# Where tiles start in SBUF: moving operands of the dense products at 0 modulo 256 bytes, small rings shortened

## The chip, the cores and the metric

The kernel runs on one NeuronCore of a Trainium2 chip. The metric is the device time of one execution in microseconds; of several executions the median counts. TensorE is called PE below, its weight loads PEld, VectorE DVE, ScalarE ACT, GpSimd POOL and SyncE SP.

## The reference

Two transformer-like blocks follow each other on 256 tokens of width 1024, batch 1, all in float32. The first block has two layers. Layer 0 joins a differential attention and a gated convolution of width 31; layer 1 joins a state-space model and a latent attention. Each layer then has a gated feed-forward part of width 2816. The second block has two layers with two streams (`x`, and a context `ctx` of 256 tokens): modulation by a conditioning vector, a windowed attention beside a grouped-query attention, a gated merge and again a gated feed-forward part.

```
def sandwich(x, g_pre, g_post, fn):
    return x + rmsnorm(fn(rmsnorm(x, g_pre)), g_post)

def swiglu(h, w_gate, w_up, w_down):
    return (jax.nn.silu(h @ w_gate) * (h @ w_up)) @ w_down

def branch_merge(ya, yb, ga, gb, w_pa, w_pb, w_o):
    merged = jax.nn.sigmoid(ga) * (ya @ w_pa) + jax.nn.sigmoid(gb) * (yb @ w_pb)
    return merged @ w_o
```

What matters here are the dense products with the weight matrices. Nearly all of PE's work is such a product of 256 tokens with a 128 x 128 piece of a weight matrix.

## The kernel before

**One dense product.** Activations lie with their features on the 128 partitions and the 256 tokens along the free axis. Weights arrive in 1 MB pieces as float32 in a ring of three `raw` tiles. `need` (line 333) cuts a piece into units of up to 128 x 1024 and splits each: ACT writes the rounded high half `uh` (line 349), DVE the rest `ul` (line 350), each in a ring of three. The activations are split likewise into a high and a low tile. `mm3` (line 363) makes one 128 x 256 output out of three matmuls of one k-tile, which the text calls a triple:

```
mm(ps, lhsT=wh, rhs=ah, start=start, stop=False)
mm(ps, lhsT=wh, rhs=al, start=False, stop=False)
mm(ps, lhsT=wl, rhs=ah, start=False, stop=stop)
```

`rhs` is the moving operand, which streams through the array; `lhsT` is the stationary operand, which a weight load brings in ahead of it. They are lines 369, 370 and 371. There are 4130 triples, and the order of the work around them is set by a table of step counts (`ORDER`) that interleaves queues of steps.

**The moving operands.** By the names in the trace: `xacth`/`xactl` (the split activations of stream x, 2192 triples), `slot` (the same for the context stream in the arena `ar`, 896), `hh`/`hl` (the hidden values of a feed-forward part, 704), `xmh`/`xml` and `xyg`/`xyn` (attention results, 256 together), `cacth` (context activations late in the second block, 48) and `nqh`, `nkvh` (34). In `token_steps` (lines 827 to 829) the roles are turned: the weights move (512 columns) and the activations are stationary.

**The rest of PE's work** is plain float32: attention scores (line 1861), transposes of probabilities (line 893), products with values (lines 901, 1891), modulation (line 1657) and statistics (lines 417, 423).

**Where a tile lies.** Tiles come from pools (`main`, `work`, `ar`, `ph`, `s5`, `ck`) that are stacked in SBUF; a tag's ring takes its place when its first tile is asked for, in steps of 32 bytes. So the start of every tile follows from the sizes and the order of all tiles asked for before it. No line of the kernel names an address.

Of the kernel before, what the change touches and what calls it, by code (L numbers as in the profile page):

```python
# [17 lines left out]
P = 128  # L18
# [134 lines left out]
class Kern:  # L153
# [20 lines left out]
    def __init__(self, ctx, tc, ins, out):  # L174
        self.ctx, self.tc, self.nc, self.ins, self.out = ctx, tc, tc.nc, ins, out
        self.cnt = 0
        self.pools = {}
        self.later, self.held, self.key = [], [], None


# [37 lines left out]
    def setup(self):  # L218
        nc, tc, ctx = self.nc, self.tc, self.ctx
        self.psum = ctx.enter_context(tc.tile_pool(name="psum", bufs=1, space=PSUM))  # L220
        ctx.callback(lambda: [self.close(k) for k in list(self.pools)[::-1]])
        self.open("main")
        self.consts = self.sb("main", "consts", [P, CBASE])
        self.vecs = self.sb("main", "vecs", [P, VSPLIT])
        self.ones = self.sb("main", "ones", [P, P])
        nc.gpsimd.memset(self.ones, 1.0)
        nc.sync.dma_start(self.consts[:, 0:P], self.ins["consts"][:, 0:P])
        nc.sync.dma_start(self.vecs[:, 0:KD], self.ins["vectors"][:, 0:KD])
        c = lambda k: self.consts[:, COFF[k][0]:COFF[k][0] + COFF[k][1]]
        self.ident, self.hsel, self.nmask = c("ident"), c("hsel"), c("nmask")  # L230
# [104 lines left out]
    def need(self, u, ahead=None):  # L335
        while self.uptr < len(self.units) and self.uptr <= u.idx + (self.UNIT_AHEAD if ahead is None else ahead):
            q = self.units[self.uptr]
            if not self.load_to(q.raw.idx):
                assert self.uptr > u.idx
                break  # L340
            self.load_to(q.raw.idx + self.RAW_AHEAD)
            self.uptr += 1
            src = q.raw.t[:, q.k0:q.k1, q.c0:q.c1]
            nk, ncol = q.k1 - q.k0, q.c1 - q.c0
            h = self.sb("main", "uh", [P, 1024], F32R, bufs=self.UNIT_BUFS)
            l = self.sb("main", "ul", [P, 1024], F32R, bufs=self.UNIT_BUFS)
            q.h = h[:, :nk * ncol].rearrange("p (k c) -> p k c", c=ncol)
            q.l = l[:, :nk * ncol].rearrange("p (k c) -> p k c", c=ncol)
            self.nc.scalar.activation(q.h, src, AF.Copy)  # L349
            self.nc.vector.tensor_tensor(q.l, src, q.h.bitcast(F32), ALU.subtract)  # L350
            self.used(q.raw)
        return u
# [48 lines left out]
    def rsqrt_small(self, ssum, n, dim, epsj=0):  # L401

        nc = self.nc
        e = lambda t: self.sb("work", "rs_" + t, [P, 16], bufs=4)[:, :n]
        v, y = e("v"), e("y0")
# [338 lines left out]
    def swiglu(self, st, wg, wu, cg, cu, wd, evacs, R=True):  # L744
# [14 lines left out]
        def rstd_a():  # L759
            st["rs"] = self.stats_a(st.pop("acc"), D)  # L760
            st["late"] = self.sb("ph", "late", [P, 2])
            self.nc.vector.tensor_copy(st["late"], st["rs"])
# [89 lines left out]
    def softmax(self, ps, groups, scale, keys, d, it, pre=None, tile=None):  # L852


        nc = self.nc
        mx = self.sb("work", "mx", [P, 2], bufs=4)[:, :groups]
        nm = self.sb("work", "nm", [P, 2], bufs=4)[:, :groups]
        sm = self.sb("work", "sm", [P, 2], bufs=8)[:, :groups]
        pt = (tile or self.w2)("prob", [P, 512])[:, :groups * keys].rearrange("p (g k) -> p g k", g=groups)
# [68 lines left out]
    def even_mixer(self, st):  # L928
# [6 lines left out]
        def begin():  # L935
            self.open("ph")
            s["C"], s["S"] = self.table("ph", "dc"), self.table("ph", "ds")
            s["u"] = self.sb("ph", "u", [P, 4, 30 + T])
            nc.gpsimd.memset(s["u"][:, :, 0:30], 0.0)
            s["cy"] = self.sb("ph", "cy", [P, 4, T])  # L940
            s["q"] = self.sb("ph", "q", [P, 4, T])
            s["k"] = self.sb("ph", "k", [P, 4, T])
            s["v"] = self.sb("ph", "v", [P, 2, 512])

        def lam():
# [3 lines left out]
            n = self.ps("n")  # L949
            nc.tensor.matmul(n[:, 0:2], lhsT=self.ones, rhs=pr, start=True, stop=True)  # L950
            e = self.sb("ph", "le", [P, 2])
# [103 lines left out]
        def weights(it):  # L1055
            K = P if it[0] == 0 else T
            self.undefer((id(d), it))
            pt, sm = d[it]
            ri = self.recip(sm)
            r1 = self.sb("work", "r1", [P, 1], bufs=2)  # L1060
            nc.vector.tensor_tensor(r1, ri[:, 1:2], s["nlam"], ALU.mult)
            wt = self.sb("work", "wt", [P, T], bufs=2)[:, :K]
            nc.vector.tensor_scalar(wt, pt[:, 1, :], r1, None, ALU.mult)
            nc.vector.scalar_tensor_tensor(wt, pt[:, 0, :], ri[:, 0:1], wt, ALU.mult, ALU.add)
            d[it] = wt
# [5 lines left out]
        def out(it):  # L1071
# [4 lines left out]
            if h == 0:  # L1076
                s["ss", qt] = self.sb("work", "ssq", [P, 4], bufs=2)
                s["ot", qt] = two("ot", [P, 512])
# [109 lines left out]
    def s5_setup(self, s):  # L1188
# [7 lines left out]
        def disc():  # L1196
# [9 lines left out]
            mag = yield from self.pexp("s5t", v, 8, "pm")  # L1206
            s["mag"] = self.sb("s5", "mag", [P, 8])
            nc.vector.tensor_copy(s["mag"], mag)
# [137 lines left out]
    def odd_mixer(self, st, s):  # L1346
# [124 lines left out]
        def glu():  # L1471
            ps = self.ps("d").rearrange("p (a t) -> p a t", a=2)
            za = [(s["zh"][:, k, :], s["zl"][:, k, :]) for k in range(2)]
            for a in range(2):
                self.dense(ps[:, a, :], [ug], za, c0=P * a)
            hb = self.sb("ph", "hb", [P, 2])
            nc.vector.tensor_scalar(hb, self.vec("l1_b_glu", 0, 2), 0.5, None, ALU.mult)
# [149 lines left out]
    def mod_setup(self):  # L1627
# [3 lines left out]
        def fn():  # L1631
            self.cs = self.sb("main", "cs", [P, KD, 32])
            nc.gpsimd.memset(self.cs, 0.0)
            t = self.sb("work", "ct", [P, 2 * KD])
            for i, n in enumerate(("c_2", "c_ctx_2")):
# [3 lines left out]
                nc.vector.tensor_tensor(self.cs[:, :, i], g, v, ALU.mult)  # L1639
            self.mods = {}  # L1640

        return [Step(fn)]

    def mod_steps(self, l):
# [4 lines left out]
        def big(c, r):  # L1649
            if c == 0:  # L1650
                m["t"] = self.mods[l] = self.sb("main", f"mod{l}", [P, 48, 2])
                m["g"] = self.mods[l, "g"] = self.sb("main", f"modg{l}", [P, 2, KD, 2])
            ps = self.ps("d")[:, :256]
# [102 lines left out]
    def proj_steps(self, st, l, rope, queries=True):  # L1756
# [22 lines left out]
        def nk(i, ps):  # L1779
            if i == 0:  # L1780
                self.new_kv(st, ("nk", "nv"))
            nc.scalar.activation(st["nk"][:, 2 * i:2 * i + 2, :], ps[0], AF.Copy)

# [274 lines left out]
    def second_block(self, X, C):  # L2058
# [6 lines left out]
        def tables(l):  # L2065
            if l == 0:
                self.open("ck", "right")
                self.new_kv(keys[0], ("gk", "gv", "nk", "nv"))
                for k in ("gk", "gv", "nk", "nv"):
                    self.unspill(keys[0], k, keys[0][k])  # L2070
# [75 lines left out]
    def prep_ctx(self, C):  # L2146
# [33 lines left out]
        def end():  # L2180
            self.spill(C, "x1", C["x"])
            C["rs1"] = self.sb("main", "crs", [P, 2])
            nc.vector.tensor_copy(C["rs1"], self.stats_a(C.pop("acc"), D))
# [46 lines left out]
    def chains(self):  # L2230
# [6 lines left out]
        self.prep_ctx(C)  # L2237
        main = [Step(lambda: self.open("work")), Step(lambda: self.open("ar"))] + self.first_block(X)
        for k in "dc":
# [32 lines left out]
```

## Time and profile before

| | us |
|---|---|
| median of 3 runs | 2039.46 (2037.99 to 2041.78) |
| the profiled execution | 2035.8 |
| its span, first to last instruction | 2034.0 |
| PE busy, share of the span | 95% |
| DVE busy | 67% |
| ACT busy | 49% |
| mean granted TensorE clock | 0.978 |

The span leaves 1.8 us of the profiled execution's own time outside. Matmuls overlap in the pipe, so a busy PE does not say at which pace they come; the distance between the starts of two matmuls does. Views that name a tile give the first and last start of a group and how many there were.

### The profile page before, as it was taken

To read this page: it belongs to the slowest core of one execution; us is meant where nothing else is said; L and a number is where in the kernel's file an instruction comes from. 1 tells how busy PE (TensorE), PEld (TensorE's weight loads), DVE (VectorE), ACT (ScalarE), POOL (GpSimd) and SP (SyncE) were. 2 spreads that over 40 slices of the span, in tenths; PEclk is the share of its full clock that TensorE was granted. 3 is DMA by queue.
4 is the path that set the end of the run, shared out by engine and by line. 5 is a ranking of instruction groups with operands and counts; after the bars stand their busy time and mean duration, and the time that the engine had idled before them with its cause. 6 is when DMAs were issued, how large, how long until landed. Compare 5 with 4: busy or idle time off the path is not lost.

```text
span 2034.0 us, 38003 instructions
## 1 busy us (share of the span) xinstructions
PE 1927.8 (95%) x15646; PEld 1785.2 (88%) x15646; DVE 1361.2 (67%) x2655; ACT 988.7 (49%) x1680; POOL 71.9 (4%) x112
## 2 busy tenths in 40 slices
PE   8889999999989999989996999989999899979998
PEld 7678889999878999789996888889999888879998
DVE  6997668777778678666655745676655755566554
ACT  5355665444445453554443455445444455535443
POOL 0212000000000000000001100000000100000000
PEclk9999999999989999999998999999999999999999
DMA  7756636666748665766556633345555643244553
GB/s 255 247 193 207 195 110 201 202 218 220 230 133 241 205 187 141 236 200 217 194 174 188 156 101 86 122 145 173 182 175 199 159 120 89 81 149 158 179 177 109
DMA packets 383775, 353.51 MB, mean 174 GB/s; under 512 B 14705, under 2 KB 370545, under 8 KB 383089
## 3 DMA queue, kind: packets, MB, share of 16 engines
q1 hardware_dynamic: 378336, 333.77, 51.9%
q0 software_dynamic: 4688, 15.73, 3.3%
q8 instruction: 123, 2.02, 0.4%
q10 hardware_dynamic: 576, 1.57, 0.2%
q14 instruction: 52, 0.42, 0.1%
HBM read 344.36 MB, written 6.68 MB: 173 GB/s over the span
## 4 chain that ended last, share of the span: by engine, by line
PE 76%; DVE 14%; ACT 4%; DMA 4%; issue 2%; SPq 0%; ACTq 0%; DVEq 0%
PE psd L369 21%; PE psd L371 20%; PE psd L370 20%; DVE ul L350 4%; PE pss L1861 4%; ACT uh L349 3%; PE pss L893 2%; PE psn L1891 2%; DMA raw<-in_w_in 2%; DVE cy L999 1%; PE psd L1657 1%; DMA raw<-in_l_w_in 1%; DMA raw<-in_w_mod 1%; PE psd L827 1%; DVE xres L592 1%
## 5 line engine op out<-in xcount | busy, mean ns | idle before, releaser
L350 DVE TENSOR_TENSOR ul<-raw,uh 128x1024 fp32r<-128x1024 f32 (+3 forms) x556 | 657.5, 1190 | 365.3 <-ACT uh L349 363.3
L349 ACT ACTIVATE uh<-raw 128x1024 fp32r<-128x1024 f32 (+3 forms) x556 | 566.0, 1025 | 337.1 <-PE psd L370 272.3
L369 PE MATMUL psd<-xacth,uh 128*128 128x256 f32 x2192 | 633.9, 289 | 9.9 <-ACT grp L703 3.1
L371 PE MATMUL psd<-xacth,ul 128*128 128x256 f32 x2192 | 626.2, 286 | 5.1 <-DVE ul L350 5.1
L370 PE MATMUL psd<-xactl,uh 128*128 128x256 f32 x2192 | 626.2, 286 | 0.6 <-DVE xactl L599 0.5
L369 PEld LDWEIGHTS psd<-xacth,uh 128*128 128x128 f32 x2192 | 425.8, 194 | 28.2 <-issue 13.4
L371 PEld LDWEIGHTS psd<-xacth,ul 128*128 128x128 f32 x2192 | 425.9, 194 | 6.6 <-DVE ul L350 6.5
L370 PEld LDWEIGHTS psd<-xactl,uh 128*128 128x128 f32 x2192 | 426.0, 194 | 1.9 <-DVE xactl L599 1.0
L369 PE MATMUL psd<-slot,uh 128*128 128x256 f32 x896 | 256.0, 286 | 0.5 <-ACT uh L349 0.5
L371 PE MATMUL psd<-slot,ul 128*128 128x256 f32 x896 | 251.4, 281 | 2.6 <-DVE ul L350 2.6
L370 PE MATMUL psd<-slot,uh 128*128 128x256 f32 x896 | 251.0, 280 | 0.0
L371 PE MATMUL psd<-hh,ul 128*128 128x256 f32 x704 | 198.1, 281 | 0.6 <-DVE ul L350 0.3
L369 PE MATMUL psd<-hh,uh 128*128 128x256 f32 x704 | 198.0, 281 | 0.0
L370 PE MATMUL psd<-hl,uh 128*128 128x256 f32 x704 | 197.5, 280 | 0.0
L369 PEld LDWEIGHTS psd<-slot,uh 128*128 128x128 f32 x896 | 169.6, 189 | 7.4 <-issue 5.2
L371 PEld LDWEIGHTS psd<-slot,ul 128*128 128x128 f32 x896 | 169.3, 189 | 3.3 <-DVE ul L350 3.3
L370 PEld LDWEIGHTS psd<-slot,uh 128*128 128x128 f32 x896 | 169.4, 189 | 0.0
L371 PEld LDWEIGHTS psd<-hh,ul 128*128 128x128 f32 x704 | 132.0, 188 | 1.6 <-DVE ul L350 1.6
L369 PEld LDWEIGHTS psd<-hh,uh 128*128 128x128 f32 x704 | 132.5, 188 | 0.4 <-issue 0.4
L370 PEld LDWEIGHTS psd<-hl,uh 128*128 128x128 f32 x704 | 132.5, 188 | 0.0
L869 ACT ACTIVATE prob<-pss,nm 128x512 f32<-128x512 f32 (+2 forms) x124 | 70.2, 568 | 22.3 <-DVE nm L879 18.9
L875 DVE TENSOR_REDUCE mx<-pss 128x1 f32<-128x512 f32 (+1 forms) x80 | 55.2, 689 | 34.4 <-PE pss L1861 33.2
(480 smaller groups left out, 2528.4 us busy)
## 6 DMA issues: line engine op xcount, KB each, us to landing
raw<-in_w_mod SPq DMA_DIRECT2D x48, 1024.0 KB, 5.5
raw<-in_w_ffn_in SPq DMA_DIRECT2D x40, 1024.0 KB, 5.1
raw<-in_w_in SPq DMA_DIRECT2D x32, 1024.0 KB, 5.7
raw<-in_w_ffn_in SPq DMA_DIRECT2D x52, 512.0 KB, 5.2
raw<-in_w_in SPq DMA_DIRECT2D x48, 512.0 KB, 5.2
raw<-in_w_ffn_out SPq DMA_DIRECT2D x24, 1024.0 KB, 4.9
raw<-in_l_w_gate SPq DMA_DIRECT2D x20, 1024.0 KB, 5.3
raw<-in_l_w_up SPq DMA_DIRECT2D x20, 1024.0 KB, 5.3
```

What stands on the lines that cost most here:

```text
L349: self.nc.scalar.activation(q.h, src, AF.Copy)
L350: self.nc.vector.tensor_tensor(q.l, src, q.h.bitcast(F32), ALU.subtract)
L369: mm(ps, lhsT=wh, rhs=ah, start=start, stop=False)
L370: mm(ps, lhsT=wh, rhs=al, start=False, stop=False)
L371: mm(ps, lhsT=wl, rhs=ah, start=False, stop=stop)
L592: nc.vector.tensor_tensor(x(m), x(m), d.pop(m), ALU.add)
L827: mm(d[i][j], lhsT=ah[:, s], rhs=u.h[:, k, :], start=kk == 0, stop=False)
L869: nc.scalar.activation(pt[:, g, :], ps[:, g, :] if one else ps[g], AF.Exp, bias=nm[:, g:g + 1], scale=scale, accum_out=sm[:, g:g + 1])
L875: nc.vector.tensor_reduce(mx, ps, AX.X, ALU.max)
L893: self.nc.tensor.transpose(t[:, k * P:(k + 1) * P], w[:, k * P:(k + 1) * P], self.ident)
L1861: nc.tensor.matmul(ps[:, a, T * i:T * i + T], lhsT=q, rhs=k, start=True, stop=True)
L1891: nc.tensor.matmul(o[64 * a:64 * a + 64, 0, g, :], lhsT=kv[kind + "v"][:, k, c:c + 64], rhs=two[a][0][:, P * i:P * i + P], start=i == 0, s ...
```

## The change

It asks for small tiles in another place and order, shortens some rings, and adds padding, so that the big tiles start elsewhere. Five small tiles move from other pools to the head of `main` (`cs`, `mag`, `crs`, the modulation tables, the rings `sm`, `mx`, `ssq`); the tile of ones shrinks from 128 columns to one, which a matmul now reads with a broadcast; `rs_a`, `rs_b`, `rs_y1`, `rs_y2` have three buffers instead of four; `r1`, `ct`, `hb` and `late` use rings of the same size that exist already; padding stands before `uh`, in `work` and in `ck`.

On all five engines the instructions stand in the same order as before, and each waits for the same counts of the same semaphores. What differs is where operands lie (and the width of one memset). From the two built programs, start address modulo 256 bytes (the moving slices are 1024 bytes apart, the stationary ones 512):

| tile | before | now |
|---|---|---|
| `uh`, `ul` (split weights) | 192 | 192 |
| `xacth`, `xactl` | 192 | 0 |
| `slot` (all), `xmh`, `xml`, `xyg`, `xyn` | 0 | 0 |
| `hh`, `hl` in layer 0 of the first block (176 triples) | 64 | 0 |
| `hh`, `hl` in layer 1 of the first block (176 triples) | 32 | 0 |
| `hh`, `hl` in the second block (352 triples) | 0 | 0 |
| `cacth`, `cactl` | 224 | 0 |
| `nqh`, `nql`, `nkvh`, `nkvl` | 32 | 0 |
| `raw` | 192 | 0 |
| rings of `work` (`w1`, `w2`, `acc`) | 224 | 0 |

Modulo 512 the split weights go from 448 to 192, `xacth` from 448 to 0, and `slot` and the second block's `hh` stay at 256.

```diff
@@ -176,6 +176,7 @@
+        self.cut = False
@@ -222,7 +223,18 @@
-        self.ones = self.sb("main", "ones", [P, P])
+        self.ones = self.sb("main", "ones", [P, 1])
+        self.cs = self.sb("main", "cs", [P, KD, 32])
+        self.mag = self.sb("main", "mag", [P, 8])
+        self.crs = self.sb("main", "crs", [P, 2])
+        self.mods = {}
+        for l in range(2):
+            self.mods[l] = self.sb("main", f"mod{l}", [P, 48, 2])
+            self.mods[l, "g"] = self.sb("main", f"modg{l}", [P, 2, KD, 2])
+        for tag, n, bufs in (("sm", 2, 8), ("mx", 2, 4), ("ssq", 4, 2)):
+            self.sb("main", tag, [P, n], bufs=bufs)
+        self.sb("main", "pad", [P, 8])
@@ -342,6 +354,10 @@
+            if self.uptr == 1 and not self.cut:
+                self.cut = True
+                self.sb("main", "upad", [P, 48])
@@ -401,7 +417,7 @@
-        e = lambda t: self.sb("work", "rs_" + t, [P, 16], bufs=4)[:, :n]
+        e = lambda t: self.sb("work", "rs_" + t, [P, 16], bufs=4 if t in ("v", "y0", "y3") else 3)[:, :n]
@@ -758,7 +774,7 @@
-            st["late"] = self.sb("ph", "late", [P, 2])
+            st["late"] = self.sb("work", "keep", [P, 2])
@@ -853,9 +869,9 @@
-        mx = self.sb("work", "mx", [P, 2], bufs=4)[:, :groups]
+        mx = self.sb("main", "mx", [P, 2], bufs=4)[:, :groups]
-        sm = self.sb("work", "sm", [P, 2], bufs=8)[:, :groups]
+        sm = self.sb("main", "sm", [P, 2], bufs=8)[:, :groups]
@@ -935,19 +951,19 @@
-            s["u"] = self.sb("ph", "u", [P, 4, 30 + T])
-            nc.gpsimd.memset(s["u"][:, :, 0:30], 0.0)
+            s["u"] = self.sb("ph", "u", [P, 4, 30 + T])
+            nc.gpsimd.memset(s["u"][:, :, 0:30], 0.0)
-            nc.tensor.matmul(n[:, 0:2], lhsT=self.ones, rhs=pr, start=True, stop=True)
+            nc.tensor.matmul(n[:, 0:2], lhsT=self.ones.to_broadcast([P, P]), rhs=pr, start=True, stop=True)
@@ -1057,7 +1073,7 @@
-            r1 = self.sb("work", "r1", [P, 1], bufs=2)
+            r1 = self.sb("main", "mx", [P, 2], bufs=4)[:, :1]
@@ -1074,7 +1090,7 @@
-                s["ss", qt] = self.sb("work", "ssq", [P, 4], bufs=2)
+                s["ss", qt] = self.sb("main", "ssq", [P, 4], bufs=2)
@@ -1204,7 +1220,7 @@
-            s["mag"] = self.sb("s5", "mag", [P, 8])
+            s["mag"] = self.mag
@@ -1473,7 +1489,7 @@
-            hb = self.sb("ph", "hb", [P, 2])
+            hb = self.sb("work", "mu", [P, 2])
@@ -1629,15 +1645,13 @@
-            self.cs = self.sb("main", "cs", [P, KD, 32])
-            t = self.sb("work", "ct", [P, 2 * KD])
+            t = self.sb("work", "rs_v", [P, 16], bufs=4)
-            self.mods = {}
@@ -1648,8 +1662,7 @@
-                m["t"] = self.mods[l] = self.sb("main", f"mod{l}", [P, 48, 2])
-                m["g"] = self.mods[l, "g"] = self.sb("main", f"modg{l}", [P, 2, KD, 2])
+                m["t"], m["g"] = self.mods[l], self.mods[l, "g"]
@@ -1779,6 +1792,8 @@
+                if st.get("pn") == "ck":
+                    self.sb("ck", "pad", [P, 248])
@@ -2066,6 +2081,7 @@
+                self.sb("ck", "pad", [P, 248])
@@ -2179,7 +2195,7 @@
-            C["rs1"] = self.sb("main", "crs", [P, 2])
+            C["rs1"] = self.crs
@@ -2235,7 +2251,7 @@
-        main = [Step(lambda: self.open("work")), Step(lambda: self.open("ar"))] + self.first_block(X)
+        main = [Step(lambda: (self.open("work"), self.sb("work", "pad", [P, 16]))), Step(lambda: self.open("ar"))] + self.first_block(X)
```

## Rows read from the trace of the kernel before

**Rows 1.** The page: span, then busy us, share, instructions of the engines.
```profile
span 2034.0 us, 38003 instructions
...
PE 1927.8 (95%) x15646; PEld 1785.2 (88%) x15646; DVE 1361.2 (67%) x2655; ACT 988.7 (49%) x1680; POOL 71.9 (4%) x112
```

**Rows 2.** The page, chain that ended last: shares by engine, then by line.
```profile
PE 76%; DVE 14%; ACT 4%; DMA 4%; issue 2%; SPq 0%; ACTq 0%; DVEq 0%
PE psd L369 21%; PE psd L371 20%; PE psd L370 20%; DVE ul L350 4%; PE pss L1861 4%; ACT uh L349 3%; PE pss L893 2%; PE psn L1891 2%; DMA raw<-in_w_in 2%; DVE cy L999 1%; PE psd L1657 1%; DMA raw<-in_l_w_in 1%; DMA raw<-in_w_mod 1%; PE psd L827 1%; DVE xres L592 1%
```

**Rows 3.** The page, costliest groups: count, busy us, mean ns, idle before.
```profile
L369 PE MATMUL psd<-xacth,uh 128*128 128x256 f32 x2192 | 633.9, 289 | 9.9 <-ACT grp L703 3.1
...
L369 PE MATMUL psd<-slot,uh 128*128 128x256 f32 x896 | 256.0, 286 | 0.5 <-ACT uh L349 0.5
...
L369 PE MATMUL psd<-hh,uh 128*128 128x256 f32 x704 | 198.0, 281 | 0.0
```

**Rows 4.** View of tile xacth, 1880:1940 (192 modulo 256): ns min/median/max, first and last start.
```profile
L371 PE MATMUL psd<-xacth,ul x168: 283/283/283, 1879.7 to 1939.8; 128*128 128x256 f32 x168
```

**Rows 5.** View of tile hh, 1982:2012, second block (0 modulo 256).
```profile
L369 PE MATMUL psd<-hh,uh x86: 279/279/279, 1981.8 to 2011.8; 128*128 128x256 f32 x86
```

**Rows 6.** View of tile slot, 639:651 (0 modulo 256).
```profile
L370 PE MATMUL psd<-slot,uh x35: 279/279/279, 638.8 to 650.8; 128*128 128x256 f32 x35
```

**Rows 7.** View of tile hh, 1064:1084, layer 1 (32 modulo 256).
```profile
L369 PE MATMUL psd<-hh,uh x56: 279/282/286, 1063.9 to 1083.7; 128*128 128x256 f32 x56
```

**Rows 8.** View of tile hh, 368:386, layer 0 (64 modulo 256).
```profile
L369 PE MATMUL psd<-hh,uh x31: 279/281/285, 367.7 to 378.4; 128*128 128x256 f32 x31
```

**Rows 9.** View of tile slot, three windows with shorter matmuls (0 modulo 256).
```profile
L370 PE MATMUL psd<-slot,uh x22: 276/276/276, 128.9 to 138.7; 128*128 128x256 f32 x22
L370 PE MATMUL psd<-slot,uh x40: 276/276/283, 534.2 to 550.8; 128*128 128x256 f32 x40
L370 PE MATMUL psd<-slot,uh x14: 276/276/276, 692.4 to 696.9; 128*128 128x256 f32 x14
```

**Rows 10.** Windows: engines busy us (count), granted clock, DMA share, GB/s.
```profile
core 0: us, PE busy (x) PEld busy (x) DVE busy (x) ACT busy (x) POOL busy (x), PEclk, DMA share, GB/s
639.00:651.00 12.00, 12.00 (x104) 12.00 (x104) 7.65 (x11) 5.75 (x9) 0.00 (x0) 1.00 0.84 229
692.60:697.00 4.40, 4.40 (x41) 4.40 (x41) 2.85 (x6) 1.98 (x2) 0.00 (x0) 1.00 0.88 247
1064.00:1084.00 20.00, 20.00 (x169) 20.00 (x168) 10.33 (x11) 9.55 (x14) 0.00 (x0) 1.00 0.52 171
1880.00:1940.00 60.00, 60.00 (x503) 60.00 (x502) 35.11 (x36) 27.26 (x32) 0.00 (x0) 1.00 0.58 190
1982.00:2012.00 30.00, 30.00 (x257) 30.00 (x256) 16.75 (x20) 12.15 (x15) 0.00 (x0) 1.00 0.50 164
```

**Rows 11.** View of line L1703 on DVE: operands at 192 (xact) and 0 (slot).
```profile
L1703 DVE SCALAR_TENSOR_TENSOR xactl<-nt,mod,xacth x32: 475/477/486, 1116.8 to 1834.3; 128x256 fp32r<-128x256 f32 x32
L1703 DVE SCALAR_TENSOR_TENSOR slot<-nt,mod,slot x16: 476/477/482, 104.8 to 631.1; 128x256 fp32r<-128x256 f32 x16
```

**Rows 12.** View of line L1861, 1200:1300 (xnk at 224).
```profile
L1861 PE MATMUL pss<-xnk,xnq x32: 376/428/480, 1234.4 to 1291.8; 64*128 64x256 f32 x32
```

**Rows 13.** View of line L1861, 1640:1780 (xnk at 0).
```profile
L1861 PE MATMUL pss<-xnk,xnq x32: 376/428/481, 1703.1 to 1758.2; 64*128 64x256 f32 x32
```

**Rows 14.** View of line L828: stationary xacth at 192, slot at 0.
```profile
L828 PE MATMUL psd<-ul,xacth x48: 387/393/504, 76.8 to 1642.4; 128*128 128x512 f32 x48
...
L828 PE MATMUL psd<-ul,slot x16: 394/394/394, 154.0 to 164.5; 128*128 128x512 f32 x16
```

**Rows 15.** DMA issues: KB each, median us from issue to landing.
```profile
slot<-sp_x POOLq DMA_DIRECT2D x1, 1024.0 KB, 7.6
cres<-sp_x POOLq DMA_DIRECT2D x1, 1024.0 KB, 5.2
```

**Rows 16.** Waits: who for whom, us in total, times, longest.
```profile
PE psd L371 <- DVE ul L350: 14.6, 23, 1.4
```


## The prediction

> **What bounds the kernel now.** Read the page's top first: PE is busy for 95% of a span of 2034.0 us, DVE for 67%, ACT for 49% [rows 1]. A busy PE is not yet the bound, so the chain of waits comes next: PE holds 76% of the work that ended last, and lines 369, 370 and 371, the three matmuls of a triple, hold 21 + 20 + 20 = 61%, or 1241 us [rows 2]. A kernel like this gets faster when a triple does. The third view is therefore that of one tile at a time, in stretches where PE never stops: divide the distance between the first and last start by the number of steps, and you have the pace of a triple, which the busy time of overlapped matmuls does not give.
>
> That view shows a difference between triples of one shape. With `xacth`, which starts at 192 modulo 256, 60.1 us / 167 = 359.9 ns [rows 4]. With `hh` of the second block, at 0, 30.0 / 85 = 352.9 ns [rows 5]; with `slot`, at 0, 12.0 / 34 = 352.9 ns [rows 6]. With `hh` of layer 1, at 32, 19.8 / 55 = 360.0 ns [rows 7]; of layer 0, at 64, 10.7 / 30 = 356.7 ns [rows 8]. Starts are rounded to 0.1 us, so a pace over 85 or more steps is good to 1 ns and one over 30 to 3 ns; the length of one matmul in the same rows says the same without that rounding: always 283 ns at 192, always 279 at 0, 279 to 286 at 32.
>
> Is it the place, or what runs beside? The windows of the same stretches [rows 10] answer: the granted clock is 1.00 in all five. `hh` at 0 keeps 353 beside a DMA share of 0.50, `slot` at 0 keeps it beside 0.84; `hh` at 32 takes 360 beside 0.52, `xacth` beside 0.58. DVE is busy 52 to 64% of each. Neither DMA nor DVE sorts the paces; the address does. `hh` is the best witness: the same lines and shape, 353 in one layer and 360 in another. It is a natural comparison and not an experiment, since `uh`, `ul` lie at 192 throughout and layers differ in other things.
>
> **The change, part by part.** The order of instructions and the waits stay, so no step, DMA or queue moves; only places do.
>
> 1. `xacth`, `xactl` from 192 to 0. 2192 triples [rows 3] x (359.9 - 352.9) = 7.0 ns: **-15.3 us**. Bounds: 0 if the address is not the cause, and with the shorter pace of item 4 throughout, about -37.
> 2. `hh` of the first block. 176 triples x (360.0 - 352.9) = -1.2 us in layer 1, 176 x (356.7 - 352.9) = -0.7 us in layer 0: **-1.9 us**.
> 3. Small ones. `cacth` (48) and `nqh`, `nkvh` (34) are too few: 82 triples x 7.1 = 0.6 us either way, taken as 0. Where the activations are the stationary operand and 512 columns of weights move, a matmul on `xacth` takes 387 to 393 ns and one on `slot` 394 [rows 14]: the move may cost up to 7 ns x 144 (48 on each of three lines) = 1.0 us, or give a little; I take **+0.6 us**.
> 4. `slot` shows a third pace in some stretches, with matmuls of 276 instead of 279 ns: 22 + 40 + 14 = 76 matmuls of one line in the three stretches of [rows 9], 8.5% of 896. In the last of them a triple takes 4.5 us / 13 = 346 ns (338 to 354 by the rounding). As 4 ns of length go with 7 of pace between 283 and 279, I estimate some 10 ns below 352.9. DMA is busiest there, 0.88 [rows 10], so it isn't quiet memory that makes it. No matmul of `xacth` or `hh` in the stretches read is under 279. If `xacth` at 0 gets it as often as `slot` does: 8.5% of 2192 = 186 x 10 = **-1.9 us** (0 to -22 if all do).
> 5. Other users of these places. On DVE the same operation takes 477 ns on `xactl` at 192 and on `slot` at 0 [rows 11]: nothing. Plain float32 scores take 428 ns with `xnk` at 224 and at 0 [rows 12, 13]: nothing. A megabyte lands in 7.6 us in `slot` at 0 and in 5.2 in `cres`, which starts at 224 [rows 15], so a place at 0 buys a DMA nothing; these two were issued at different times, so the 2.4 us is no price. `raw` at 0: 0, bounds +3 and -3 us, from the same two rows over the few loads that the chain shows at its start and end.
> 6. Shorter rings and shared ones. A ring that is too short shows as a new wait. Each engine waits for the same counts as before, so there is none: 0. The memset of one column instead of 128 is done once at the start: 0.
>
> Sum over PE: -15.3 - 1.9 + 0.6 + 0 - 1.9 = -18.5 us. Not all of it lies on the path. All 4130 triples at some 357 ns are 1474 us, of which the chain holds 1241, or 84%; elsewhere DVE, ACT or a DMA end last, and a quicker triple only waits longer. What is late next is the split of weights: PE waits for `ul` 23 times, 14.6 us [rows 16], and that grows where triples outrun DVE. 0.84 x 18.5 = **-15.6 us**. The profiled execution took 2035.8 us (the span and 1.8 us around it): 2020.2. The median of the three runs stands 3.7 us above it, which I add: **2023.9 us**, call it 2024.
>
> [...]
>
> **The rivals.**
>
> *A, nothing happens.* The pace belongs to what `xacth` and the early `hh` do (when they were written, what loads beside them), and not to where they lie. For it: no row has one tile at two places in one layer. Against it: [rows 5, 7] and the windows. Price: items 1, 2 and 4 fall away; **2039.5**, perhaps half a microsecond more. [...]
>
> *B, the short pace spreads.* `xacth` shares `slot`'s residue; if half of its triples fall into the pace of item 4, 1096 x 10 x 0.84 = 9 us go as well, less the 1.6 already counted: about **2016**; if all do, 2007.
>
> *C, the gain is taken back.* DVE writes `ul` no faster, and half-clock stretches or the float32 work do not shrink. If only a third of the sum reaches the end, -6 us: **2033**. For it: 16% of the triples are off the chain already, and the wait of [rows 16]. Against it: DVE is busy 50 to 64% in the dense stretches [rows 10], so it has room for a 2% quicker PE.
>
> *D, slower: the period is 512 bytes and not 256.* The change also takes the weights from 448 to 192 modulo 512. From weights to `xacth` the distance is then 320, as it was for `slot`; but `slot` (896 triples), the attention results (256) and the second block's `hh` (352), which stay at 256, come to a distance of 64, and so does the first block's `hh` (352). No dense row at 353 has that distance. If those 1504 + 352 lose p ns each against 352.9, the change loses 1504 p + 352 (p - 5.4), 5.4 being what item 2 would have won on average, and wins 17.2 - 0.6 = 16.6. It breaks even at p = 10. With the 7.1 ns of [rows 7] it still wins some 4 us on the path; at twice that, 14.2 ns, it loses 21.4 + 3.1 - 16.6 = 7.9, x 0.84 = 6.6 us: **2046**. Against it: successive k-tiles step by 1024 bytes in the moving operand and 512 in the weights, so bits above the period asked about change all the time, and the matmuls of [rows 4, 5] stay at 283 and 279 ns to the last; and none of the dense stretches read has a pace above 360.
>
> **How the numbers follow.** Forecast (2019 to 2029, from the bounds of items 3 to 6 and a path share of 0.6 to 1): 0.70. B 0.10, C 0.06, A 0.07, D 0.07, of which some 0.03 near no change and 0.04 slower. A measurement of this kernel tells 0.2%, or 4.1 us, from no change. Faster by more: forecast, B and C, 0.86. Within it: A and the middle of D, 0.10. Slower: 0.04. The range goes from 2012, which holds half of B, to 2032, which takes in the better half of C; A, D, the rest of B and of C lie outside, less than 0.2 together.
>
> **What would show it.** Right: matmuls on `xacth` of 279 ns (the median of its stretches was 283) and triples near 353; `hh` of the first block at 279; the same granted clock; the wait for `ul` up by a few microseconds at most. B: 276 on `xacth` for more than a tenth of them. C: the pace falls and the end does not, with waits for DVE grown by 8 us or more. A: 283 stays on `xacth` at its new place. D: `slot` and the late `hh` above 279, at 283 or more. The forecast is wrong if `xacth` stays above 357 ns, or if `slot` and `hh` leave 353.

## The result

| | before | changed | ratio, 95% interval |
|---|---|---|---|
| median of 4 runs, us | 2039.17 | 2021.73 | 0.9914 (0.9897 to 0.9931) |
| profiled execution, us | 2035.8 | 2022.4 | |

The changed kernel is 17.4 us faster by the medians and 13.4 us by the two profiled executions; the interval, as a share of 2039, is 14 to 21 us. Forecast was 2024 us. The mean granted clock was 0.978 in the profiled execution of before and is 0.975 in this one: 91 us of the first trace and 104 us of the second lie at the lower of its two levels (0.50, where the rest has 1.00), so part of what separates 13.4 from 17.4 us can be the clock of these two executions; that is an argument and no measurement.

Page of the changed kernel (span; busy time, share and instructions of the engines; then the chain that ended last by engine and by line; then two of the costliest groups):

```profile
span 2020.5 us, 38003 instructions
...
PE 1914.1 (95%) x15646; PEld 1767.9 (87%) x15646; DVE 1360.2 (67%) x2655; ACT 989.9 (49%) x1680; POOL 73.4 (4%) x112
...
PE 76%; DVE 14%; ACT 4%; DMA 4%; issue 2%; SPq 0%; ACTq 0%; DVEq 0%
PE psd L385 21%; PE psd L387 20%; PE psd L386 20%; DVE ul L366 4%; PE pss L1876 4%; ACT uh L365 3%; PE pss L909 2%; PE psn L1906 2%; DMA raw<-in_w_in 2%; PE psd L1670 1%; DVE cy L1015 1%; DMA raw<-in_l_w_in 1%; DMA raw<-in_w_mod 1%; PE psd L843 1%; PE psd L844 1%
...
L385 PE MATMUL psd<-xacth,uh 128*128 128x256 f32 x2192 | 626.0, 286 | 12.9 <-ACT grp L719 5.9
...
L385 PE MATMUL psd<-hh,uh 128*128 128x256 f32 x704 | 197.3, 280 | 0.0
```

Lines 385 to 387 are lines 369 to 371 of before. The counts, the shares of the chain and the share of PE are those of [rows 1, 2]; what changed is the mean of a matmul on `xacth`, 289 to 286 ns, and on `hh`, 281 to 280 [rows 3]. Nothing in the make-up of the chain shows the gain: a chain of the same pieces got shorter.

The view of one tile shows it (ns minimum/median/maximum of one matmul, first and last start); `xacth` late in the second block, `hh` of layer 1 and of layer 0 of the first block, `slot`:

```profile
L387 PE MATMUL psd<-xacth,ul x165: 279/279/279, 1867.9 to 1925.8; 128*128 128x256 f32 x165
...
L385 PE MATMUL psd<-hh,uh x58: 279/279/279, 1055.7 to 1075.9; 128*128 128x256 f32 x58
...
L387 PE MATMUL psd<-hh,ul x36: 279/280/280, 365.7 to 378.3; 128*128 128x256 f32 x36
...
L386 PE MATMUL psd<-slot,uh x41: 279/279/279, 633.8 to 647.9; 128*128 128x256 f32 x41
```

`xacth` at its new place: 57.9 us / 164 = 353.0 ns where [rows 4] had 359.9. `hh` of layer 1: 20.2 / 57 = 354, where [rows 7] had 360.0. `slot` did not move: 14.1 / 40 = 352.5, as [rows 6]. The 12.6 us of `hh` of layer 0 hold one pause of 0.2 us, so they give no pace; the steps around it are 353 or 354 ns. The windows of the first and last of these stretches (busy us of the engines, granted clock, DMA share, GB/s) are like those of [rows 10]:

```profile
core 0: us, PE busy (x) PEld busy (x) DVE busy (x) ACT busy (x) POOL busy (x), PEclk, DMA share, GB/s
634.00:648.00 14.00, 14.00 (x121) 14.00 (x120) 9.70 (x14) 7.36 (x11) 0.00 (x0) 1.00 0.76 221
1868.00:1926.00 58.00, 58.00 (x495) 58.00 (x494) 35.18 (x36) 26.83 (x32) 0.00 (x0) 1.00 0.58 191
```

Counted over the starts of the whole trace, in triples that nothing interrupted: 1554 of `xacth` take 352.1 ns on average, where 1546 took 359.7; 157 of the 1554 have the short pace of 340 of which item 4 spoke. All 2900 or so such triples together: 356.6 ns before, 352.4 now. (A looser count takes every triple whose matmuls and the next triple's first start less than 130 ns apart. It finds 1988 and 1984 of `xacth`, with 352.0 and 359.7 ns and 196 short ones; all of them together 356.8 and 352.4.) The last view is that of the waits (who for whom, us in total, times, longest), in answer to [rows 16]:

```profile
PE psd L387 <- DVE ul L366: 16.3, 25, 1.2
```

### The profile page after: what moved, and what is told of

Read it like the earlier page. It is cut to its first block, busy times and chain, and to the rows that moved or that the text cites. A ratio compares the mean times of both kernels' runs of the same rounds, so it can differ in the third digit from the quotient of the medians.

```text
span 2020.5 us, 38003 instructions
## 1 busy us (share of the span) xinstructions
PE 1914.1 (95%) x15646; PEld 1767.9 (87%) x15646; DVE 1360.2 (67%) x2655; ACT 989.9 (49%) x1680; POOL 73.4 (4%) x112
## 4 chain that ended last, share of the span: by engine, by line
PE 76%; DVE 14%; ACT 4%; DMA 4%; issue 2%; SPq 0%; ACTq 0%; DVEq 0%
PE psd L385 21%; PE psd L387 20%; PE psd L386 20%; DVE ul L366 4%; PE pss L1876 4%; ACT uh L365 3%; PE pss L909 2%; PE psn L1906 2%; DMA raw<-in_w_in 2%; PE psd L1670 1%; DVE cy L1015 1%; DMA raw<-in_l_w_in 1%; DMA raw<-in_w_mod 1%; PE psd L843 1%; PE psd L844 1%
## 5 line engine op out<-in xcount | busy, mean ns | idle before, releaser
L385 PE MATMUL psd<-xacth,uh 128*128 128x256 f32 x2192 | 626.0, 286 | 12.9 <-ACT grp L719 5.9
L387 PE MATMUL psd<-xacth,ul 128*128 128x256 f32 x2192 | 617.7, 282 | 6.9 <-DVE ul L366 6.9
L386 PE MATMUL psd<-xactl,uh 128*128 128x256 f32 x2192 | 616.8, 281 | 0.4 <-DVE xactl L615 0.3
L385 PEld LDWEIGHTS psd<-xacth,uh 128*128 128x128 f32 x2192 | 416.7, 190 | 31.5 <-issue 14.7
L387 PEld LDWEIGHTS psd<-xacth,ul 128*128 128x128 f32 x2192 | 416.8, 190 | 8.9 <-DVE ul L366 8.9
L386 PEld LDWEIGHTS psd<-xactl,uh 128*128 128x128 f32 x2192 | 417.0, 190 | 1.8 <-DVE xactl L615 0.9
L472 DVE TENSOR_TENSOR acc<-acc,sq 128x256 f32<-128x256 f32 x116 | 49.1, 424 | 44.5 <-ACT sq L471 42.7
```

What stands on the lines that cost most here:

```text
L472: self.nc.vector.tensor_tensor(acc, acc, s, ALU.add)
```

## The experiments

Two theories explain the paces of before equally well. **M** (moving): the place of the moving operand decides, as the prediction had it. **R** (relative): the distance from the weights to the moving operand, modulo 256, decides. All weights lay at 192, so no row of before could tell a place from a distance. **N** is rival A: neither.

### The pairing by itself

The kernel of this run has 16 moving tiles and 16 tiles of weights, and nothing else runs:

```
for rw in ("000", "032", ... "224"):          # start of the weights modulo 256
    for rx in ("000", "032", ... "224"):      # start of the moving operand
        40 triples: wh x xh, wh x xl, wl x xh, over four k-tiles
```

> A kernel of its own, which computes nothing of the reference: eight pairs of moving tiles and eight pairs of split weight tiles start at 0, 32, ... 224 modulo 256, and each of the 64 pairings runs 40 triples (three float32r matmuls of 128x128 by 128x256, as in the dense products) with nothing else running. Theory M (the place of the moving operand alone): one pace per place of the moving tiles, whatever the weights: about 353 ns at 0, 360 at 32 and 192, 356 at 64, 350 at 224. Theory R (the distance from the weights, modulo 256): one pace per distance: about 360 at 0 and 96, 353 at 64, 356 at 128, 350 at 32, since the weights lay at 192 in every row so far. Theory N (neither; the pace belongs to what runs beside): one pace for all 64.

One row of the map is the changed kernel's own place of the weights, 192. View of the lines, forms apart (count, busy us, mean ns of one, idle before):

```profile
L27 PE MATMUL ps<-x000h,w192h 128*128 128x256 f32 x40 | 11.2, 279 | 0.0
...
L27 PE MATMUL ps<-x032h,w192h 128*128 128x256 f32 x40 | 11.3, 282 | 0.0
...
L27 PE MATMUL ps<-x064h,w192h 128*128 128x256 f32 x40 | 11.3, 281 | 0.0
...
L27 PE MATMUL ps<-x096h,w192h 128*128 128x256 f32 x40 | 11.2, 280 | 0.0
...
L27 PE MATMUL ps<-x128h,w192h 128*128 128x256 f32 x40 | 11.0, 276 | 0.0
...
L27 PE MATMUL ps<-x160h,w192h 128*128 128x256 f32 x40 | 11.2, 281 | 0.0
...
L27 PE MATMUL ps<-x192h,w192h 128*128 128x256 f32 x40 | 11.3, 283 | 0.0
...
L27 PE MATMUL ps<-x224h,w192h 128*128 128x256 f32 x40 | 11.2, 280 | 0.0
...
L27 PE MATMUL ps<-x192h,w000h 128*128 128x256 f32 x40 | 11.1, 276 | 0.0
...
L27 PE MATMUL ps<-x192h,w128h 128*128 128x256 f32 x40 | 11.2, 280 | 0.0
...
L27 PE MATMUL ps<-x192h,w224h 128*128 128x256 f32 x40 | 11.2, 281 | 0.0
```

With the weights fixed (the first eight lines) the mean goes from 276 to 283 ns by the moving operand's place, beside nothing at all. With the moving operand fixed at 192 (the seventh line and the last three) it goes over the same range by the place of the weights: 283 at distance 0, 276 at 192, 280 at 64, 281 at 224. From the starts of the trace (us per pairing / triples), the whole map says which of the two counts. Mean ns of a triple, at each distance (moving operand minus weights, modulo 256) for weights at 32 to 224; weights at 0 read alike but for the first pairing (matmuls of 299 to 304 ns), where the kernel starts up:

| distance | 0 | 32 | 64 | 96 | 128 | 160 | 192 | 224 |
|---|---|---|---|---|---|---|---|---|
| least of the pairings | 359.8 | 353.4 | 353.3 | 359.7 | 355.9 | 351.9 | 340.2 | 354.9 |
| greatest | 359.8 | 353.5 | 353.5 | 360.0 | 356.2 | 356.0 | 353.3 | 355.1 |

By distance the rows of the map coincide, but for 192 and 160, where some pairings have a second pace (at 160 one of eight, 356 against 352); by place a column runs through all eight paces. This is R. It gives every row of before: `xacth` at 192 lay at distance 0, 360; `slot` and late `hh` at 64, 353; `hh` at 32 and 64 lay at 96 and 128, 360 and 356. And it shows a place that the change does not use: at distance 192 five of eight pairings run at 340, three at 353.

### Two cross-checks in the kernel

First, the activations put back, and with them `raw` and the residual `xres`, which lie behind the same padding; everything else is left as the change has it:

```diff
-        self.sb("main", "pad", [P, 8])
+        self.sb("main", "pad", [P, 56])
...
-                self.sb("main", "upad", [P, 48])
```

> The changed kernel with xacth, xactl (and raw, xres) put back at 192 modulo 256 by a larger padding ahead of them; the weights stay at 192, everything else where the change put it, and the shorter rings stay. Theories M and R: xacth triples return to 360 ns, 2192 x 7.6 ns (352.1 measured in the changed kernel) x 0.84 = 14 us are lost: 2036 us, ratio to the kernel before 0.998. Theory N, or the shorter rings and other tiles did it: 2022 us as the changed kernel, ratio 0.991.

Ratio 0.9984 (0.9965 to 1.0004). View of tile `xacth`, late, and of `hh` in layer 1:

```profile
L386 PE MATMUL psd<-xacth,ul x167: 283/283/283, 1879.9 to 1939.7; 128*128 128x256 f32 x167
...
L386 PE MATMUL psd<-hh,ul x57: 280/280/280, 1065.9 to 1085.7; 128*128 128x256 f32 x57
```

`xacth` is at 283 ns again (59.8 / 166 = 360.2 a triple), `hh` still at 280. Of the gain of 0.86%, 0.70% went with what was put back (0.86% - 0.16%), or 14.3 us: the 14 expected for the activations (the part of `raw` in it is small, see item 5 below). What the shorter rings and all other tiles do together is what remains, 0.16%, which the interval does not tell from nothing.

Second, the moving operands left at 0, and the weights moved:

```diff
-            if self.uptr == 1 and not self.cut:
-                self.cut = True
-                self.sb("main", "upad", [P, 48])
+            first, self.cut = not self.cut, True
             h = self.sb("main", "uh", [P, 1024], F32R, bufs=self.UNIT_BUFS)
             l = self.sb("main", "ul", [P, 1024], F32R, bufs=self.UNIT_BUFS)
+            if first:
+                self.sb("main", "utail", [P, 48])
```

> The changed kernel with the split weights uh, ul at 0 modulo 256 instead of 192 (their padding goes behind them); all moving operands stay at 0. Theory M: no change from the changed kernel, 2022 us, ratio 0.991, matmuls of 279 ns. Theory R: the distance is 0 everywhere as it was for xacth before, all 4130 triples take 360 ns: 4130 x 7.5 x 0.84 = 26 us more, 2048 us, ratio 1.004, matmuls of 283 ns.

Ratio 1.0031 (1.0018 to 1.0043): slower than before, though every moving operand lies at 0 modulo 256. View of tiles `xacth` and `hh`:

```profile
L386 PE MATMUL psd<-xacth,ul x167: 283/283/283, 1889.9 to 1949.7; 128*128 128x256 f32 x167
...
L384 PE MATMUL psd<-hh,uh x79: 283/283/283, 1999.8 to 2027.9; 128*128 128x256 f32 x79
```

283 ns on both, 359.7 a triple over the whole trace. From the changed kernel that is +7.3 ns x 4130 = 30 us of PE, of which 1.17%, 24 us, reached the end. M falls, R holds.

### The short pace in the kernel

If distance decides, 192 is worth trying: the weights at 64.

```diff
...
-                self.sb("main", "upad", [P, 48])
+                self.sb("main", "upad", [P, 16])
...
+                self.sb("main", "utail", [P, 32])
```

> The changed kernel with the split weights at 64 modulo 256, so that the distance from the weights to every moving operand is 192 (it is 64 in the changed kernel). Theory R with the map: undisturbed triples at 340 ns. If all are, 4130 x 12 ns x 0.84 = 42 us less than the changed kernel: 1980 us, ratio to the kernel before 0.971. If the pace falls into 353 as often as in the map (3 of 8 pairings), 26 us less: 1996 us, ratio 0.979. If DVE and the other waits take half of it back, 2001 us. If 340 needs an idle memory, or theory R is wrong: 2022 us, ratio 0.991.

Ratio 0.9831 (0.9801 to 0.9861), some 17 us better than the changed kernel; 59% of the undisturbed triples of the traced execution run at 340 ns, the mean is 345.4. That is one execution; the times of the six go from 1996.7 to 2016.4 us. Where the pace is short it holds (view of tile `xacth`; 55.8 us / 164 triples = 340.2):

```profile
L388 PE MATMUL psd<-xacth,ul x165: 276/276/277, 1848.0 to 1903.8; 128*128 128x256 f32 x165
```

### Finer than 32 bytes

Two more kernels measured pairings by themselves. In one the moving operand goes through 64 distances of 4 bytes, then eight distances come back 16 times, each behind a stall.

> A kernel of its own, which computes nothing of the reference. First 40 triples for each of 64 distances from weights to moving operand, in steps of 4 bytes, without a pause; then 16 times the eight distances in steps of 32 bytes, 12 triples each, with PE made to wait for ACT before each group. Theory R says that the first part repeats the map at each multiple of 32; if what counts is a bank of 32 bytes or more, paces between are steps or slopes between the neighbours, and if single words count, they jump. The second part: if 340 and 353 at distance 192 are two states that a stall picks between, both appear over its 16 groups, and at 64 too (one in ten triples of the changed kernel had 340 there); if the neighbour in the program decides, each distance has one pace.

The paces jump from word to word. At 0, 4, 8, 12, 16: 360, 370, 360, 352, 350 ns. At 108, 112, 116: 360, 340, 365. Only 112, 144 and 192 ran at 340. After stalls distance 192 gave 340 in 10 groups and 353 in 6, so these are two states that a stall picks between; 64 gave 353 in all 16, 0 gave 360 in all 16. Distances 32 (349 or 353) and 160 (352 or 356) have two states as well.

The other varied the distance of the high part (which streams in two of the three matmuls) and that of the low part apart.

> A kernel of its own, which computes nothing of the reference. First 256 pairings, 16 triples each: the distance of the high part and that of the low part of the moving operand from their weights, each in steps of 16 bytes. Then eight distances (0, 16, 28, 32, 64, 112, 144, 192), common to both parts, 24 times with a stall of PE ahead of 12 triples. [...] If the pace were set by something slower than the streams (issue, loading), no pairing would be under 340.

No pairing of the 256 is below 340, and only that of 112 with 112 is at it. A mixture of the paces of the two distances fits some pairings: high part at 144 with low part at 0 took 347, which is (2 x 340 + 360) / 3 with the 340 that 144 had in the run above (alone it takes 356 here). It fails in others: high part at 112 with low part at 64 took 360, where 112 alone takes 340 and 64 alone 353. After 24 stalls 112 gave 340 to 343 every time, 144 gave 350 or 356, 192 gave 340 in 15 and 353 in 9, and 64, which had one state above, gave 340 once.

Which state a stall picks is hardly chance in these two runs. PE waited for one, two or three copies of ACT in turn, and at distance 192 the length of that wait sorts the groups. In the first run the 6 groups at 353 are those behind the shortest wait (0.8 us from the last start before it to the first behind it), and the 10 at 340 those behind 1.2 and 1.6 us. In the second run all 8 groups behind the middle wait (1.1 to 1.2 us) had 353, and 15 of the 16 behind a shorter or a longer one had 340. One length, 0.8 us, picked 353 in one run and 340 in the other, so the length alone does not say which.

So 112 looked like the place without the second state. For the kernel the weights had to go to 144, a multiple of 16 only, and so into one tile:

```diff
...
-            h = self.sb("main", "uh", [P, 1024], F32R, bufs=self.UNIT_BUFS)
-            l = self.sb("main", "ul", [P, 1024], F32R, bufs=self.UNIT_BUFS)
+            if first:
+                self.sb("main", "upad", [P, 32])
+                self.upair = self.sb("main", "upair", [P, 4 + 2 * self.UNIT_BUFS * 1024], F32R)
+                self.sb("main", "utail", [P, 8])
+            b = (self.uptr - 1) % self.UNIT_BUFS
+            h = self.upair[:, 4 + 1024 * b:4 + 1024 * (b + 1)]
+            l = self.upair[:, 4 + 1024 * (self.UNIT_BUFS + b):4 + 1024 * (self.UNIT_BUFS + b + 1)]
```

> The changed kernel with the split weights at 144 modulo 256, so that the distance from the weights to every moving operand is 112, the one that kept 340 to 343 ns after each of 24 stalls. A multiple of 16 and not of 32 needs an offset inside a tile, so the six buffers of uh and ul are cut from one tile; 28 of the waits on each of ACT and DVE for smaller units are then some matmuls earlier. Theory R: undisturbed triples at 340 to 343 ns and none at 353. Against the changed kernel 4130 x 11 ns, times 0.84 to 0.6 (the share that the run with weights at 64 kept): 38 to 27 us less, 1984 to 1995 us, ratio 0.973 to 0.978. If beside real work the pace falls into 353 as at 192: 0.983. If theory R is wrong: 0.991.

A miss: ratio 1.0007 (0.9988 to 1.0026), no triple at 340, 358.3 on average. View of tile `hh`, late:

```profile
L387 PE MATMUL psd<-hh,upair x84: 284/284/285, 1993.9 to 2023.8; 128*128 128x256 f32 x84
```

29.9 us / 83 = 360 ns, where the changed kernel has 353. The control has the same tile and waits with the weights at 192 (pad of 40, offset of 8 floats):

> The control for the run with weights at 144: the same single tile and the same waits, weights at 192 modulo 256 as in the changed kernel (distance 64). Theory R: 353 ns and the changed kernel's time, ratio 0.991. If the earlier release of buffers is what helps, the ratio is that of the run at 144.

Ratio 0.9899 (0.9877 to 0.9921), 351.7 ns: the changed kernel again. The tile is not the cause of the miss; the place is.

What differs between the kernel and the measurement is which operand was moved to 16 modulo 32. So one more measurement, with the real layout (eight k-tiles, the low weights 12288 bytes behind the high ones), moved the weights in steps of 4 bytes, and then the other operand:

> A kernel of its own, which computes nothing of the reference, in the layout of the real one (eight k-tiles, low weights 12288 bytes behind the high ones). The run with weights at 144 had 359 ns at distance 112, where two measurements by themselves, which moved the other operand, had 340. First the moving operand stays at 0 and the weights move by 4 bytes at a time (64 places, 32 triples each); then the weights stay and the moving operand moves by 16 bytes, with the low part 8192 bytes behind the high one (0 modulo 512, as xacth and xactl); then the same with 256 more between them; then the weights in steps of 16 bytes, each 12 times after a stall. Theory A: off multiples of 32 it counts which of the two is moved: the weights at 144 give 359, the moving operand at 112 gives 340. Theory B: it counts how the low part lies to the high one modulo 512: 359 at 112 with 0 between them, 340 with 256. Theory C: only work on other engines makes 359: 340 in all three parts.

View of line 26, the matmuls, in three stretches: weights at 144 with the moving operand at 0; weights at 76; weights at 0 with the moving operand at 112 (the extremes belong to the neighbouring pairings):

```profile
L26 PE MATMUL psa<-x,w x98: 277/284/285, 419.0 to 430.6; 128*128 128x256 f32 x98
...
L26 PE MATMUL psa<-x,w x99: 276/276/284, 225.8 to 237.0; 128*128 128x256 f32 x99
...
L26 PE MATMUL psa<-x,w x98: 275/275/283, 817.9 to 828.9; 128*128 128x256 f32 x98
```

At one distance, 112, the weights moved give 284 ns and 360.0 a triple, the other operand moved 275 and 340.0. With 256 bytes more between high and low part, paces are the same in all 16 places. Theory A: in multiples of 32 the distance is enough, finer than that, as at 112, both places count. With the moving operand at 0 the weights ran at 340 at 52, 64, 76 and 88; after 12 stalls the place 64 held 340 each time, here without a second state.

### The four places

The last three kernels are that at 144 with other pads and offsets: 8 and 5 floats (52), 16 and 3 (76), 16 and 6 (88).

> The changed kernel with the split weights at 52 modulo 256 (one tile, as in the run at 144), one of four places at which the measurement by itself gave 340 ns to every triple after the first nine. If that measurement carries over, as it did at 64 and 144: undisturbed triples at 340 in half or more, ratio about 0.983 as with the weights at 64; if in all, 4130 x 12 x 0.84 = 42 us less than the changed kernel, ratio 0.971. If the short pace is lost at each wait and does not come back, 0.991.

> As the run at 52, with the weights at 76 modulo 256: 0.983 with half of the undisturbed triples at 340 ns, 0.971 with all, 0.991 where each wait loses the short pace.

> As the run at 52, with the weights at 88 modulo 256: 0.983 with half of the undisturbed triples at 340 ns, 0.971 with all, 0.991 where each wait loses the short pace.

All runs of the kernel together, by the mean pace of the triples that nothing interrupted:

| weights at | pace, ns | at 340 | ratio to before (95% interval) |
|---|---|---|---|
| 0 | 359.7 | 0 | 1.0031 (1.0018 to 1.0043) |
| 144 | 358.3 | 0 | 1.0007 (0.9988 to 1.0026) |
| 192, before | 356.6 | 3% | 1 |
| 192, activations back | 356.3 | 3% | 0.9984 (0.9965 to 1.0004) |
| 192, changed | 352.4 | 7% | 0.9914 (0.9897 to 0.9931) |
| 192, one tile | 351.7 | 13% | 0.9899 (0.9877 to 0.9921) |
| 64 | 345.4 | 59% | 0.9831 (0.9801 to 0.9861) |
| 88 | 344.4 | 59% | 0.9777 (0.9748 to 0.9805) |
| 52 | 343.3 | 79% | 0.9787 (0.9760 to 0.9813) |
| 76 | 341.5 | 91% | 0.9741 (0.9710 to 0.9773) |

A straight line through the ten, with ratios taken times 2040 us, has a slope of 3.2 us per ns, against 4130 triples x 1 ns = 4.13: 0.78 of what a triple gains reaches the end, and no kernel lies more than 4.4 us off the line. The pace is that of one traced execution and the ratio that of all, so some scatter is to be expected. The weights at 76 beat both kernels: 1988.0 us, 2.6% under before and 1.7% under the change. Its chain and one of its stretches of `xacth`:

```profile
span 1991.6 us, 38003 instructions
...
PE 77%; DVE 13%; DMA 4%; ACT 4%; issue 2%; SPq 0%; ACTq 0%; DVEq 0%
PE psd L387 21%; PE psd L389 20%; PE psd L388 20%; DVE upair L368 4%; PE pss L1878 4%; ACT upair L367 3%; PE pss L911 2%; DMA raw<-in_w_in 2%; PE psn L1908 2%; DVE cy L1017 2%; PE psd L1672 2%; PE psn L435 1%; DMA raw<-in_l_w_down 1%; PE psd L845 1%; PE psn L1911 1%
...
L389 PE MATMUL psd<-xacth,upair x165: 276/276/276, 1840.0 to 1895.7; 128*128 128x256 f32 x165
```

55.7 us / 164 = 339.6 ns. PE still ends last in 77% of the span, so the next step is still the triple.

## Why the prediction was right, and where not

**The pace of `xacth`** (item 1). 359.9 to 352.9 was forecast, 359.7 to 353 in nine triples of ten was measured, and putting the activations back took 14.3 us of the gain with it. The size was right. The cause was not: "the address does", said the prediction, and meant the moving operand's own place. It did say that the weights lay at 192 throughout, but drew a rival from it (D) only for a period of 512. The runs put the distance to the weights there. That the forecast came out all the same was luck: the change left the weights at 192. With them at 0 the same argument would have promised 353 ns and a ratio of 0.991, and the run had 360 ns and 1.003.

**`hh`** (item 2): 360.0 (layer 1) and 355.9 ns (layer 0) became 353.4 in the whole trace, as forecast.

**The small ones** (item 3). The median of line 828 on `xacth` [rows 14] went from 393 to 394 ns; the 0.6 us were too much, by less than can be measured. `cacth` stayed at 351 on average.

**The short pace** (item 4). 8.5% of the triples was forecast, 10% came (157 of 1554), and one is 13 ns short and not 10. That the share came out is luck. The 8.5% counted three stretches, whose 76 matmuls include some of 279 ns and more [rows 9]; in the whole trace of before, 132 of the 896 matmuls of line 370 on `slot` take 276 ns (15%), and in that of the change, with `slot` at the same place and distance, 49 (5%). So place alone does not set the share. Of rival B, that the short pace spreads, the sign (276 ns on more than a tenth of `xacth`) stands on its edge, 206 of 2192 matmuls on line 385 and 226 on line 387; its price, half of them, did not come. At other distances it did (91% with the weights at 76).

**Other users** (item 5). The prediction took nothing for `raw`, and that was wrong for a load and as good as right for the kernel. The 512 KB loads of `w_in` into `raw` landed sooner at 0 modulo 256 than at 192. DMA issues of the changed kernel, then of the kernel with `raw` back at 192 (KB each, median us to landing):

```profile
raw<-in_w_in SPq DMA_DIRECT2D x48, 512.0 KB, 4.7
raw<-in_w_ffn_out SPq DMA_DIRECT2D x24, 1024.0 KB, 4.7
```

```profile
raw<-in_w_in SPq DMA_DIRECT2D x48, 512.0 KB, 5.3
raw<-in_w_ffn_out SPq DMA_DIRECT2D x24, 1024.0 KB, 5.1
```

Half a microsecond for a load of 512 KB of `w_in`, in all eight kernels with `raw` at 0 (4.7 or 4.8) against the two at 192 (5.2 before and 5.3). The 1 MB loads of `w_ffn_out` separate less: 4.7 to 4.9 at 0, 4.9 before and 5.1. The pair in [rows 15] pointed the other way and was no price. For the time of the kernel the place of `raw` is worth little: the two kernels with `raw` at 192 lie 2.9 and 0.6 us above the line through the ten, the eight others 0.4 below it on average, and the scatter is as large.

**Shorter rings** (item 6): no new wait shows, and the run with the activations back leaves 0.16% for them and all else.

**The sum.** Forecast was -18.5 us on PE. Measured: 356.6 to 352.4 is 4.2 ns x 4130 = -17.3. Of that 0.84 was to reach the end; 0.78 does. 17.3 x 0.78 = 13.5 us. The two profiled spans (2034.0 and 2020.5) differ by as much, but at unequal clocks, so that is no proof; the medians differ by 17.4, with an interval that begins at 14. The chances that the prediction left outside its range add up to 0.22 (A and D 0.14, half of B 0.05, half of C 0.03) and not to less than 0.2.

**The rivals.** A (nothing happens) falls with the two cross-checks and with the map: with nothing else running, the same three matmuls took 340 to 360 ns as the distance of the two operands changed, at a granted clock of 0.998. C (the gain is taken back) priced a loss of two thirds; 22% is missing on the line through the ten. The wait for `ul` grew from 14.6 to 16.3 us only. Where the rest goes was not traced; stretches in which PE does not end last are a guess that nothing here shows. D (a period of 512) is out: `slot` and late `hh`, from distance 320 to 64 modulo 512, kept 279 ns. It asked the right question, the distance, with the wrong period.

**Still open.** Why one distance is better than another: the runs varied where the two operands lie and show no cause. How a stall picks one state or the other: its length matters, but at distance 192 the measurements gave 340 in 10 of 16, 15 of 24 and 12 of 12 groups, the kernel in 59% of its triples. And why, below 32 bytes, it matters which of the two is moved.

## What to carry to other kernels

Take the pace of matmuls from their starts, one operand at a time, in stretches without a pause: two paces for one shape are time that no engine's busy share shows (here 360 and 353 ns on `xacth`, with PE busy for 95% of both spans). Where a natural comparison varies one thing, ask what it holds fixed; here it held the weights, and "at 0" was "64 from the weights". Measure the pairing by itself before padding, in the real layout and with the same operand moved, since a padding that is right for one place of the weights is a loss for another (ratio 0.991 with the weights at 192 and 1.003 with them at 0), and any later change of a tile's size moves both.

## What the runs showed of the hardware

- The pace of matmuls with a weight load before each went by the distance between the weights and the moving operand in SBUF: three float32r matmuls of 128x128 by 128x256 took 340 to 360 ns in steps of 32 bytes, and up to 370 at steps of 4, beside nothing else. No pairing of the 64, 64, 256 and 96 averaged below 340.
- Some pairings had two lasting paces (340 and 353 at distance 192), and a stall changed from one to the other. Its length sorted them: at 192, 353 behind 0.8 us and 340 behind 1.2 and 1.6 us in one run, in the other 353 behind 1.1 to 1.2 us and 340 behind all but one of the shorter and longer stalls.
- A 512 KB load of `w_in` into SBUF landed in 4.7 to 4.8 us at 0 modulo 256 and in 5.2 to 5.3 at 192; loads of 1 MB of `w_ffn_out` in 4.7 to 4.9 and 4.9 to 5.1.
- One distance was fast or slow by which operand lay off a multiple of 32: at 112, 340 ns with the moving operand off it and 360 with the weights.
